# Low-rank decay columns appended to the first head's value weights, with another order of the first loads and splits

## The chip, the cores and the metric

The kernel runs on one NeuronCore of a Trainium2 chip. The metric is the device time of one execution in microseconds (us). The kernel before was timed three times, and its median counts; one further execution was recorded by the hardware profiler, and all views of the trace come from that one. Engines are named as the profile names them: PE (TensorE, with PEld for its weight loads), ACT (ScalarE), DVE (VectorE), POOL (GpSimd) and SP (SyncE, which here only issues DMA transfers).

## The reference

One encoder layer in float32 on 1024 tokens of width 1024. Only the beginning matters here: the norm, the combined input projection and the decays that come from its 32 low-rank columns.

```python
h = rmsnorm(x, norm_mix[l])
proj = h @ w_in[l]
q, k, v, r, lr_f, lr_b, u, g_a, g_b = jnp.split(proj, split_points, axis=-1)
log_a_f = log_sigmoid(lr_f @ w_decay_up_fwd[l] + b_decay_fwd[l]) / GATE_NORMALIZER
log_a_b = log_sigmoid(lr_b @ w_decay_up_bwd[l] + b_decay_bwd[l]) / GATE_NORMALIZER
...
o = o_fwd + o_bwd          # gated linear attention, 4 heads, forward and backward
...
x = x + merged @ w_out[l]
h2 = rmsnorm(x, norm_ffn[l])
gate, up = jnp.split(h2 @ w_ffn_in[l], 2, axis=-1)
x = x + (jax.nn.silu(gate) * up) @ w_ffn_out[l]
return rmsnorm(x, norm_final)
```

q and k are 512 wide (4 heads of 128), v is 1024 wide (4 heads of 256), lr_f and lr_b are 16 wide each.

## The kernel before

**Products.** Float32 accuracy comes from three products of numbers in a shorter format (fp32r). Every operand is split into a high part (`hi`, a cast by ACT) and a low part (`lo`, the difference, by DVE or POOL), by `split_to`; `mm3` then issues hi·hi, hi·lo and lo·hi, and calls `pump`, which lets work that was put aside (splits of coming weights, transposes, norms) be issued between matmuls after so much matmul time. There is no scheduler: each engine runs its instructions in the order in which the program issues them.

**The start.** Tokens come in eight tiles of 128. For each tile `norm_x` squares and sums on ACT, adds epsilon on DVE, takes the power −1/2 on POOL (`rms_scale`) and scales the tile on DVE (`xn`). PE transposes `xn` into banks `tr`; `gain_and_split` then takes each pair of feature blocks out with the gain `g_mix`, hi part `hh` by ACT, lo part `hl` by DVE. These are the feature-major activations `hT`, in two halves of 512 tokens. The gains and biases of all vectors come as 40 rows of 128 numbers (`rows`), loaded by six DMAs, and are turned into columns (`cols`) by one PE transpose (`vps`) and one DVE copy.

**Values of the first head.** `values` makes one token tile: 8 blocks of k, three matmuls each, the stationary operand a token tile of `hT`, the moving one 256 columns of weights (`wh`, `wl`). The weights come in four tiles `raw` of two k blocks each; each is split while the first pairs of features are made, ACT's cast of one raw tile standing between two pairs. The low part of the first is DVE's, those of the other three are POOL's. The loop goes over tiles two at a time, with norms and transposes of later tiles between the matmuls.

**Low-rank columns.** After the eight value tiles come 32 matmuls of 512 columns (line 449): the moving operand is `hh` or `hl` of 512 tokens, the stationary one `lw`, in which the 32 low-rank weight columns stand four times, three times as hi and once as lo. That gives `lrT`, feature-major with 128 rows; its third copy is replaced by its own lo part. `up` holds the up-projections in four bands that fit, so that one product `up`·`lrT` has the hi and lo terms (line 640, used by the attention of each head). Between these 32 matmuls the weights of the first head's q are split. Then come q and k of the first head, 512 tokens a time, its attention, and the rest of the layer.

**Buffers and queues.** All loads are issued by SP, in order. A DMA's completion is counted on one of eight semaphores in turn, so a ninth load waits for the first to have landed. The four `raw` buffers are used again by the weights of q and k, once they are split. PSUM has three banks for matmul results and five for transposes, `z` and others.

Of the kernel before, what the change touches and what calls it, by code (L numbers as in the profile page):

```python
# [10 lines left out]
F32 = mybir.dt.float32  # L11
# [6 lines left out]
P = 128  # L18
# [8 lines left out]
RANK = 16  # L27
CH = 128
# [23 lines left out]
def kernel(  # L52
# [38 lines left out]
    def name(s):  # L91
        count[0] += 1
        return f"{s}_{count[0]}"
# [140 lines left out]

    order = []
# [108 lines left out]
    vec_rows = [(norm_mix, 8), (norm_ffn, 8), (gla_norm, 8), (pool_scale, 8), (b_decay_fwd, 4), (b_decay_bwd, 4)]  # L344
    n_rows = sum(n for _, n in vec_rows)
    rows = tmp.tile([n_rows, P], F32, tag="t2", name="rows")
# [6 lines left out]
    def load_rows(at, v, n):  # L353
        nc.sync.dma_start(rows[at : at + n, :], v[0].rearrange("(j p) -> j p", p=P))
# [6 lines left out]
    load_rows(0, *vec_rows[0])  # L361
    load_x(1)
    for i in range(1, len(vec_rows)):
        load_rows(sum(n for _, n in vec_rows[:i]), *vec_rows[i])
    fetch()
    for t in (2, 3):
        load_x(t)
    nc.sync.dma_start(lraw[:, :, :], w_in[:, LR0:U0].rearrange("(k p) c -> p k c", p=P))
# [20 lines left out]

    lw = [wts.tile([P, 4, 4, 2 * RANK], F32R, tag="wh", name=name("lw")) for _ in range(2)]
    up = slot(F32R, (HEADS, 2, DK), "up")

    def low_rank_weights():
        for i in range(2):
            raw = lraw[:, 4 * i : 4 * i + 4, :]
            nc.scalar.copy(lw[i][:, :, :3, :], raw.unsqueeze(2).broadcast_to([P, 4, 3, 2 * RANK]))
            nc.vector.tensor_tensor(lw[i][:, :, 3, :], raw, as_f32(lw[i][:, :, 0, :]), op=ALU.subtract)  # L400
        nc.scalar.copy(up[:, :, :, :], uraw[:, :, :, :])
        nc.vector.tensor_tensor(up[32:64], uraw[32:64], as_f32(up[32:64]), op=ALU.subtract)
# [8 lines left out]
    nc.tensor.transpose(vps[:, :n_rows], rows[:, :], ident[:n_rows, :n_rows])  # L411
    cols = const.tile([P, n_rows], F32, tag="cols", name="cols")
    nc.vector.tensor_copy(cols[:, :], vps[:, :n_rows])
    g_mix, g_ffn, g_gla, g_pool = (cols[:, 8 * i : 8 * i + 8] for i in range(4))
    b_dec = (cols[:, 32:36], cols[:, 36:40])
# [5 lines left out]
    prepare()  # L421
    for kp, ps in enumerate(trs):
        pending.pop(0)()
        gain_and_split(ps, kp, 0, hT, g_mix)
    w = take(ahead=False)
    norm_x(2)
    norm_x(3)
    for t in range(0, NT, 2):
        if t + 4 < NT:
            begin(norms(t + 4), 1)  # L430
        if t == 2:
            for d, w_up in enumerate((w_decay_up_fwd, w_decay_up_bwd)):
# [6 lines left out]
        values(w, v, t + 1)  # L439
        finish_side()  # L440
        if t == 4:
            low_rank_weights()
    prepare()
    lrT = slot(F32R, (2, HALF), "lrT")
    for half in range(2):
        ps = bank(ps_mm)
        for k in range(KT):
            for i in range(2):
                nc.tensor.matmul(
                    ps[:, :], lw[k // 4][:, k % 4, :, :].rearrange("p a r -> p (a r)"), hT(k, half)[i],  # L450
                    start=k == 0 and i == 0, stop=k == KT - 1 and i == 1,
                )
            pump(2 / 3)
        nc.scalar.copy(lrT[:, half, :], ps[:, :])
        nc.vector.tensor_tensor(lrT[64:96, half, :], ps[64:96, :], as_f32(lrT[64:96, half, :]), op=ALU.subtract)
# [1389 lines left out]
```

## Time and profile before

| | |
|---|---|
| median of three runs | 1403.24 us (1403.14 to 1404.75) |
| the profiled execution's own time | 1401.25 us |
| its span, first to last instruction | 1399.5 us |
| granted TensorE clock, mean | 0.997 |
| DMA traffic | 243.62 MB, mean 174 GB/s |

In the profile a row of a timeline gives start, duration, engine, line, operation, out<-in with the program's names, shape and count; in brackets stands how long the engine had been idle and what ended that. A row of the windows view gives the length of a stretch and the busy time of each engine in it. Line numbers are those of the kernel before.

### The profile page before, as it was taken

To read this page: it belongs to the slowest core of one execution; us is meant where nothing else is said; L and a number is where in the kernel's file an instruction comes from. 1 tells how busy PE (TensorE), PEld (TensorE's weight loads), DVE (VectorE), ACT (ScalarE), POOL (GpSimd) and SP (SyncE) were. 2 spreads that over 40 slices of the span, in tenths; PEclk is the share of its full clock that TensorE was granted. 3 is DMA by queue.
4 is the path that set the end of the run, shared out by engine and by line. 5 is a ranking of instruction groups with operands and counts; after the bars stand their busy time and mean duration, and the time that the engine had idled before them with its cause. 6 is when DMAs were issued, how large, how long until landed. Compare 5 with 4: busy or idle time off the path is not lost.

```text
span 1399.5 us, 18553 instructions
## 1 busy us (share of the span) xinstructions
PE 1369.9 (98%) x6677; PEld 1155.1 (83%) x6677; DVE 843.4 (60%) x1073; ACT 624.1 (45%) x1119; POOL 749.3 (54%) x558
## 2 busy tenths in 40 slices
PE   7999999999999999999999999999999999999997
PEld 6889898988888888788887888888888888888876
DVE  6266757667734885587874865556565556343363
ACT  6364655554333444455346633333333334443253
POOL 3251626142288455568665176666666667454354
PEclk9999999999999999999999999999999999999999
DMA  6212413222377678897424555554444447976461
GB/s 193 76 45 62 136 45 122 91 76 75 122 237 235 208 231 250 317 412 284 157 76 174 172 180 174 173 173 156 144 142 149 140 154 254 387 257 219 165 227 75
DMA packets 167613, 243.62 MB, mean 174 GB/s; under 512 B 10937, under 2 KB 98017, under 8 KB 167521
## 3 DMA queue, kind: packets, MB, share of 16 engines
q1 hardware_dynamic: 155104, 216.23, 46.2%
q10 hardware_dynamic: 12416, 26.22, 5.1%
q8 instruction: 52, 0.85, 0.2%
q14 instruction: 41, 0.33, 0.1%
HBM read 164.55 MB, written 77.86 MB: 173 GB/s over the span
## 4 chain that ended last, share of the span: by engine, by line
PE 69%; DVE 4%; DMA 2%; issue 2%; POOL 2%; ACT 1%; ACTq 0%; SPq 0%; POOLq 0%; DVEq 0%
PE ps L271 67%; DMA u_out<-uph 1%; POOL wl L198 1%; PE tp L959 0%; DMA gor<-g_out 0%; DMA wor<-t_out 0%; DVE upl L585 0%; PE op L800 0%; DMA ph<-p_out 0%; DVE x L1523 0%; PE yb L271 0%; POOL n3rs L1506 0%; POOL mg L1150 0%; POOL gl L1439 0%; ACT wh L197 0%
## 5 line engine op out<-in xcount | busy, mean ns | idle before, releaser
L198 POOL TENSOR_TENSOR wl<-fs,wh 128x512 fp32r<-128x512 f32 x120 | 164.8, 1377 | 165.7 <-ACT wh L197 141.8
L271 PE MATMUL ps<-gl,wh 128*128 128x512 f32 x616 | 239.8, 389 | 0.8 <-DVE gl L1439 0.8
L271 PE MATMUL ps<-gh,wh 128*128 128x512 f32 x616 | 240.3, 390 | 0.0
L271 PE MATMUL ps<-gh,wl 128*128 128x512 f32 x616 | 239.7, 389 | 0.0
L198 POOL TENSOR_TENSOR wl<-fraw,wh 128x512 fp32r<-128x512 f32 x90 | 129.3, 1437 | 65.1 <-ACT wh L197 64.4
L198 POOL TENSOR_TENSOR ol<-gor,oh 128x1024 fp32r<-128x1024 f32 (+1 forms) x42 | 100.2, 2392 | 93.0 <-ACT oh L197 70.3
L271 PE MATMUL ps<-hh,wh 128*128 128x512 f32 x376 | 149.4, 397 | 0.0
L271 PE MATMUL ps<-hh,wl 128*128 128x512 f32 x376 | 146.8, 390 | 0.0
L271 PE MATMUL ps<-hl,wh 128*128 128x512 f32 x376 | 146.5, 390 | 0.0
L198 POOL TENSOR_TENSOR wl<-raw,wh 128x512 fp32r<-128x512 f32 x47 | 64.7, 1391 | 146.4 <-ACT wh L197 135.5
L271 PEld LDWEIGHTS ps<-gl,wh 128*128 128x128 f32 x616 | 115.7, 188 | 24.9 <-DVE gl L1439 1.3
L271 PEld LDWEIGHTS ps<-gh,wl 128*128 128x128 f32 x616 | 115.7, 188 | 24.1
L271 PEld LDWEIGHTS ps<-gh,wh 128*128 128x128 f32 x616 | 115.7, 188 | 23.6
L271 PE MATMUL ps<-oh,oh 128*128 128x512 f32 x308 | 119.9, 389 | 1.1 <-DVE x L1767 1.1
L271 PE MATMUL ps<-ol,oh 128*128 128x512 f32 x308 | 119.9, 389 | 0.2 <-DVE ol L198 0.2
L271 PE MATMUL ps<-oh,ol 128*128 128x512 f32 x308 | 119.8, 389 | 0.0
L198 POOL TENSOR_TENSOR wl<-wraw,wh 128x512 fp32r<-128x512 f32 x56 | 90.2, 1637 | 46.7 <-ACT wh L197 46.6
L198 DVE TENSOR_TENSOR ol<-wor,oh 128x1024 fp32r<-128x1024 f32 (+1 forms) x42 | 61.7, 1489 | 54.0 <-ACT oh L197 45.2
L197 ACT CAST wh<-fs 128x512 fp32r<-128x512 f32 x120 | 73.8, 615 | 31.0 <-DVE fs L869 24.2
L271 PEld LDWEIGHTS ps<-hh,wl 128*128 128x128 f32 x376 | 70.6, 188 | 15.2
L271 PEld LDWEIGHTS ps<-hh,wh 128*128 128x128 f32 x376 | 70.8, 188 | 13.5
L271 PEld LDWEIGHTS ps<-hl,wh 128*128 128x128 f32 x376 | 70.7, 188 | 13.6
(251 smaller groups left out, 3181.1 us busy)
## 6 DMA issues: line engine op xcount, KB each, us to landing
fraw<-in_w_ffn_in_dram SPq DMA_DIRECT2D x44, 512.0 KB, 5.9
gor<-g_out SPq DMA_DIRECT2D x35, 512.0 KB, 6.4
raw<-in_w_in_dram SPq DMA_DIRECT2D x48, 256.0 KB, 3.4
g_out<-s SPq DMA_DIRECT2D x44, 256.0 KB, 2.3
fraw<-in_w_in_dram SPq DMA_DIRECT2D x20, 512.0 KB, 5.4
wor<-t_out SPq DMA_DIRECT2D x20, 512.0 KB
g_out<-g SPq DMA_DIRECT2D x33, 256.0 KB, 2.6
x<-in_x_dram SPq DMA_DIRECT2D x16, 512.0 KB, 5.2
```

The source lines that it names most:

```text
L197: nc.scalar.copy(hi, src)
L198: eng.tensor_tensor(lo, src, as_f32(hi), op=ALU.subtract)
L271: nc.tensor.matmul(ps, a[i], b[j], start=first and n == 0, stop=last and n == 2, skip_group_check=onto)
```

## The change

The 32 low-rank columns are appended to the 256 value columns of the first head. A class `FirstWeights` holds four tile pairs (`fwh`, `fwl`) of two k blocks by 288 columns; `split_values` fills the first 256 columns from `raw`, `split_low` the last 32 from `lraw`, all on POOL. Each value tile is then one product of 288 columns. Its last 32 are copied by ACT, four times side by side, to `low_rows`, token-major. When q has begun, eight transposes (`transpose_low`) bring them into the layout of `lrT`, whose third copy is then treated as before. The 32 matmuls of line 449, `lw` and `low_rank_weights` are gone.

The first weights and the low-rank columns are loaded right after the second x tile, ahead of the third and fourth; the five vectors other than `norm_mix` come after these. `norm_mix` has a transpose of its own (8 columns), the others a second one (32 columns) after the first value tile. All four weight casts stand ahead of the feature scalings on ACT. The low parts of the first two weight tiles are DVE's, those of the other two POOL's. `up` has three bands filled and the fourth left at zero. The first weights of q are fetched in the loop over the tiles and prepared for splitting after tile 5.

```diff
+    class FirstWeights(Weights):
+        def __init__(self, tiles, low):
+            self.per, self.low = 2, low
+            self.todo = tiles
+            self.parts = [tuple(slot(F32R, (2, VL), s) for s in ("fwh", "fwl")) for _ in tiles]
+        def split_values(self, i, eng):
+            split_to(*(t[:, :, :DV] for t in self.parts[i]), self.todo[i][:, :, :], eng)
+        def split_low(self):
+            for i, (hi, _) in enumerate(self.parts):
+                nc.gpsimd.tensor_copy(hi[:, :, DV:], self.low[:, 2 * i : 2 * i + 2, :])
+            for i, (hi, lo) in enumerate(self.parts):
+                nc.gpsimd.tensor_tensor(
+                    lo[:, :, DV:], self.low[:, 2 * i : 2 * i + 2, :], as_f32(hi[:, :, DV:]), op=ALU.subtract
+                )
...
     load_x(0)
-    load_rows(0, *vec_rows[0])
+    load_rows(rows[0], 0, norm_mix, 8)
     load_x(1)
-    for i in range(1, len(vec_rows)):
-        load_rows(sum(n for _, n in vec_rows[:i]), *vec_rows[i])
-    fetch()
+    first_raw = load(*next(order))
+    nc.sync.dma_start(lraw[:, :, :], w_in[:, LR0:U0].rearrange("(k p) c -> p k c", p=P))
     for t in (2, 3):
         load_x(t)
-    nc.sync.dma_start(lraw[:, :, :], w_in[:, LR0:U0].rearrange("(k p) c -> p k c", p=P))
+    for i, (v, n) in enumerate(vec_rows):
+        load_rows(rows[1], sum(n for _, n in vec_rows[:i]), v, n)
...
+    def first_values(w, v, t):
+        ps = bank(ps_mm)
+        for kt in range(KT):
+            mm3(ps[:, :VL], tokens(hT(kt, t // 4), t), w(kt), kt == 0, kt == KT - 1)
+        split_to(*(part[:, t % 4, :] for part in v[t // 4]), ps[:, :DV])
+        nc.scalar.copy(low_rows[:, t, :, :], ps[:, DV:VL].unsqueeze(1).broadcast_to([P, 4, 2 * RANK]))
+    def transpose_low(t):
+        half, i = t // 4, t % 4
+        if i == 0:
+            low_banks[half] = bank(ps_g, "lt")
+        ps = low_banks[half]
+        nc.tensor.transpose(ps[:, i * P : (i + 1) * P], low_rows[:, t, :, :].rearrange("p a r -> p (a r)"), ident[:, :])
+        if i == 3:
+            nc.scalar.copy(lrT[:, half, :], ps[:, :])
+            nc.vector.tensor_tensor(lrT[64:96, half, :], ps[64:96, :], as_f32(lrT[64:96, half, :]), op=ALU.subtract)
...
-    prepare()
+    w = FirstWeights(first_raw, lraw)
+    w.split_low()
+    for i in range(KT // 2):
+        w.split_values(i, nc.vector if i < 2 else nc.gpsimd)
     for kp, ps in enumerate(trs):
-        pending.pop(0)()
         gain_and_split(ps, kp, 0, hT, g_mix)
-    w = take(ahead=False)
...
         if t == 2:
             for d, w_up in enumerate((w_decay_up_fwd, w_decay_up_bwd)):
-                for i in range(4):
+                for i in range(3):
                     load_up(i, d, w_up)
-        values(w, v, t)
+            fetch()
+        first_values(w, v, t)
         finish_side()
+        if t == 0:
+            vectors(1, 8)
...
         if t == 4:
-            low_rank_weights()
-    prepare()
...
-    for half in range(2):
-        ps = bank(ps_mm)
-        for k in range(KT):
-            for i in range(2):
-                nc.tensor.matmul(
-                    ps[:, :], lw[k // 4][:, k % 4, :, :].rearrange("p a r -> p (a r)"), hT(k, half)[i],
-                    start=k == 0 and i == 0, stop=k == KT - 1 and i == 1,
-                )
-            pump(2 / 3)
...
+            up_weights()
+            prepare()
+    soon(1, *(partial(transpose_low, t) for t in range(NT)))
```

SP's queue before, from its fourth load on (`rows` the vectors, `raw` the first weights, `x` token tiles, `lraw` the low-rank columns):

```order
L354 DMA rows<-in_norm_ffn_dram 8x128
L354 DMA rows<-in_gla_norm_dram 8x128
L354 DMA rows<-in_pool_scale_dram 8x128
L354 DMA rows<-in_b_decay_fwd_dram 4x128
L354 DMA rows<-in_b_decay_bwd_dram 4x128
L205 DMA raw_145<-in_w_in_dram 128x2x256
L205 DMA raw_147<-in_w_in_dram 128x2x256
L205 DMA raw_149<-in_w_in_dram 128x2x256
L205 DMA raw_151<-in_w_in_dram 128x2x256
L351 DMA x_128<-in_x_dram 128x1024
L351 DMA x_129<-in_x_dram 128x1024
L368 DMA lraw_136<-in_w_in_dram 128x8x32
```

The same place in the change:

```order
L206 DMA raw_141<-in_w_in_dram 128x2x256
L206 DMA raw_143<-in_w_in_dram 128x2x256
L206 DMA raw_145<-in_w_in_dram 128x2x256
L206 DMA raw_147<-in_w_in_dram 128x2x256
L384 DMA lraw_137<-in_w_in_dram 128x8x32
L371 DMA x_128<-in_x_dram 128x1024
L371 DMA x_129<-in_x_dram 128x1024
L374 DMA rows<-in_norm_ffn_dram 8x128
L374 DMA rows<-in_gla_norm_dram 8x128
L374 DMA rows<-in_pool_scale_dram 8x128
L374 DMA rows<-in_b_decay_fwd_dram 4x128
L374 DMA rows<-in_b_decay_bwd_dram 4x128
```

The weights and `lraw` moved ahead of the x tiles and the vectors; `lraw` is the eighth load and no longer the fifteenth.

POOL before, from the power of the second token tile on (`n1rs` the powers, `wl` low parts of the first weights):

```order
L303 TENSOR_TENSOR n1rs_177<-n1rs_177,half_neg 128x1
L198 TENSOR_TENSOR wl_213<-raw_147,wh_212 128x512
L198 TENSOR_TENSOR wl_223<-raw_149,wh_222 128x512
L198 TENSOR_TENSOR wl_233<-raw_151,wh_232 128x512
L303 TENSOR_TENSOR n1rs_244<-n1rs_244,half_neg 128x1
```

And in the change (`fwh`, `fwl` the widened weights):

```order
L323 TENSOR_TENSOR n1rs_179<-n1rs_179,half_neg 128x1
L249 CAST fwh_204<-lraw_137 128x2x32
L249 CAST fwh_206<-lraw_137 128x2x32
L249 CAST fwh_208<-lraw_137 128x2x32
L249 CAST fwh_210<-lraw_137 128x2x32
L251 TENSOR_TENSOR fwl_205<-lraw_137,fwh_204 128x2x32
L251 TENSOR_TENSOR fwl_207<-lraw_137,fwh_206 128x2x32
L251 TENSOR_TENSOR fwl_209<-lraw_137,fwh_208 128x2x32
L251 TENSOR_TENSOR fwl_211<-lraw_137,fwh_210 128x2x32
L199 TENSOR_TENSOR fwl_209<-raw_145,fwh_208 128x2x256
L199 TENSOR_TENSOR fwl_211<-raw_147,fwh_210 128x2x256
L323 TENSOR_TENSOR n1rs_254<-n1rs_254,half_neg 128x1
```

Between the powers of the second and the third token tile stand eight small operations and two splits, where three splits stood.

PE before, from the end of the last value tile on (`ps_599` that tile, `ps_631` the low-rank product, whose rows go on to 32 matmuls):

```order
L271 MATMUL ps_599<-wh_232,hh_465 128x256
L271 MATMUL ps_599<-wl_233,hh_465 128x256
L271 MATMUL ps_599<-wh_232,hl_466 128x256
L449 MATMUL ps_631<-hh_206,lw_157 128x512
L449 MATMUL ps_631<-hl_207,lw_157 128x512
```

And in the change (`ps_620` the last value tile, `ps_683` the first half of q, `lt` the transposes of the low rows `lr`):

```order
L291 MATMUL ps_620<-fwh_210,hh_482 128x288
L291 MATMUL ps_620<-fwl_211,hh_482 128x288
L291 MATMUL ps_620<-fwh_210,hl_483 128x288
L291 MATMUL ps_683<-hh_228,wh_613 128x512
L291 MATMUL ps_683<-hl_229,wh_613 128x512
L291 MATMUL ps_683<-hh_228,wl_614 128x512
L429 MATMUL lt_687<-ident,lr_158 128x128 x4
L429 MATMUL lt_694<-ident,lr_158 128x128 x4
```

The value matmuls are 288 columns wide, q follows them directly, and the eight transposes stand after q's first three matmuls.

More of the change, by code (lines that the diff above doesn't have):

```diff
@@ L410, with vectors @@
     vps = bank(ps_g, "vps")
[L411 to L415, printed above, removed]
+    cols = [const.tile([P, n], F32, tag=f"cols{n}", name=f"cols{n}") for n in (8, n_rows)]
+    def vectors(i, at):
+        n = cols[i].shape[1]
+        nc.tensor.transpose(vps[:, at : at + n], rows[i][:, :], ident[:n, :n])
+        nc.vector.tensor_copy(cols[i][:, :], vps[:, at : at + n])
+    vectors(0, 0)
+    g_mix = cols[0]
+    g_ffn, g_gla, g_pool = (cols[1][:, 8 * i : 8 * i + 8] for i in range(3))
+    b_dec = (cols[1][:, 24:28], cols[1][:, 28:32])
     norm_x(1)
```

24 lines of the change are left out of this document (10 added, 14 removed).

## The prediction

> **What bounds the kernel now.** I read the page first, for the share of each engine and the chain that ended last.
>
> ```profile
> PE 1369.9 (98%) x6677; PEld 1155.1 (83%) x6677; DVE 843.4 (60%) x1073; ACT 624.1 (45%) x1119; POOL 749.3 (54%) x558
> PE 69%; DVE 4%; DMA 2%; issue 2%; POOL 2%; ACT 1%; ACTq 0%; SPq 0%; POOLq 0%; DVEq 0%
> ```
>
> TensorE (PE) is busy for 98% of the span, so what shortens the time must remove TensorE time or TensorE waiting. The idle rest is 29.6 us (1399.5 less 1369.9). Next the windows view, by stage (values of the first head, the low-rank product, q and k of the first head); after the stretch, a column each for PE, PEld, DVE, ACT and POOL, then clock and DMA.
>
> ```profile
> 10.80:18.70 7.90, 5.70 (x32) 4.61 (x30) 5.28 (x13) 7.87 (x18) 4.89 (x5) 1.00 0.78 235
> 18.70:43.40 24.70, 24.70 (x211) 24.70 (x212) 17.09 (x41) 16.17 (x39) 2.19 (x4) 1.00 0.33 95
> 43.40:50.70 7.30, 7.30 (x34) 6.06 (x33) 1.11 (x2) 2.00 (x4) 2.58 (x2) 1.00 0.14 37
> 50.70:72.90 22.20, 22.20 (x99) 18.40 (x98) 0.69 (x1) 4.66 (x9) 5.08 (x4) 1.00 0.37 107
> ```
>
> From 18.7 to 72.9 us TensorE never idles, with the other engines far below it: each nanosecond taken from its queue there comes off the end. Before 18.7 it waits for others. So the change has two halves: arithmetic on a full engine, and a new order of loads and splits in a stage that others bound.
>
> **The arithmetic.** The low-rank product is 32 matmuls of 512 columns. The timeline gives starts, which I use for pitch, since the busy times of neighbours overlap. These are the first and last of 41 consecutive value matmuls, the first and last of the 32, and what followed.
>
> ```profile
> 38.40 0.28 PE L271 MATMUL ps<-wh,hh 128*128 128x256 f32 x1
> 43.20 0.28 PE L271 MATMUL ps<-wl,hh 128*128 128x256 f32 x1
> 43.44 0.40 PE L449 MATMUL ps<-hh,lw 128*128 128x512 f32 x1
> 50.50 0.39 PE L449 MATMUL ps<-hl,lw 128*128 128x512 f32 x1
> 50.72 0.39 PE L271 MATMUL ps<-hh,wh 128*128 128x512 f32 x1
> ```
>
> Removed: 50.72 − 43.44 = 7.28 us, 0.2275 us each. A 256-column matmul starts every 4.80/40 = 0.120 us.
>
> Added, first term: 8 token tiles x 8 k x 3 products = 192 value matmuls grow from 256 to 288 columns. No row shows 288. The two pitches give a slope of (0.2275 − 0.120)/256 = 0.42 ns a column, so 32 columns cost 13.4 ns and 192 of them 2.58 us. The ends: nothing, if the pitch of 0.120 hides some width, and 192 x (0.2275 − 0.120) = 20.6 us, if 288 cost what 512 do. I take 2.58, since 288 lies close to 256 and a straight line joins the two rows; below nothing is excluded, as a wider matmul streams more columns.
>
> Added, second term: eight 128x128 transposes of the token-major low rows, right after the first three q matmuls. Four such transposes between matmuls look like this:
>
> ```profile
> 33.34 0.29 PE L271 MATMUL ps<-wh,hl 128*128 128x256 f32 x1
> 33.46 0.60 PE L318 MATMUL tr<-ident,xn 128*128 128x128 f32 x4
> 33.81 0.36 PE L271 MATMUL ps<-wh,hh 128*128 128x256 f32 x1
> 34.02 0.28 PE L271 MATMUL ps<-wl,hh 128*128 128x256 f32 x1
> ```
>
> They hold the queue for 0.35 us, and the next matmul takes 0.21 instead of 0.12, so eight in a row cost 2 x 0.35 + 0.09 = 0.79 us. The last one waits for ACT's copy of the last tile's columns, behind that tile's values cast, which before stood here:
>
> ```profile
> 43.64 0.37 ACT L197 CAST vh<-ps 128x256 fp32r<-128x256 f32 x1 [2.51 <-PE ps L271]
> 44.61 1.29 POOL L198 TENSOR_TENSOR wl<-raw,wh 128x512 fp32r<-128x512 f32 x1 [16.94 <-ACT wh L197]
> ```
>
> Cast and copy need about 0.7 us from the last values matmul; three q matmuls (0.68 us) and seven transposes (0.61 us) stand before the transpose that waits, so it is covered.
>
> TensorE's sum: −7.28 + 2.58 + 0.79 = −3.91 us.
>
> The low-rank stage was also cover for splitting q's first weights. The change puts that split into tiles 6 and 7 of the values (24 x 0.133 = 3.2 us each), where POOL is idle (2.19 us busy of 24.70). Its loads go out ahead of tile 2. Cost nothing; without that cover q would wait for one POOL split, 2.5 us by the second row (44.61 + 1.29 − 43.40). The eight ACT copies, the casts of the transposed rows and the split of the up weights lie under 16.17 of 24.70 us of ACT; nothing. SP issues six small uraw loads instead of eight, ahead of weights that nobody awaits; nothing.
>
> **The start.** The next rows are SP's issues, then ACT, DVE, POOL and PE up to where TensorE runs full.
>
> ```profile
> 0.80 0.39 SPq L351 DMA_DIRECT2D x<-in_x_dram  x1
> 2.06 0.34 SPq L354 DMA_DIRECT2D rows<-in_norm_ffn_dram  x1
> 4.51 2.75 SPq L205 DMA_DIRECT2D raw<-in_w_in_dram  x4
> 8.28 0.43 SPq L368 DMA_DIRECT2D lraw<-in_w_in_dram  x1
> 6.38 1.06 ACT L311 ACTIVATE xn<-x 128x1024 f32<-128x1024 f32 x1 [0.72 <-DMA x<-in_x_dram]
> 9.92 0.84 ACT L325 ACTIVATE hh<-tr,cols 128x256 fp32r<-128x256 f32 x2 [0.99 <-PE tr L318]
> 10.64 0.62 ACT L197 CAST wh<-raw 128x512 fp32r<-128x512 f32 x1
> 14.34 1.10 ACT L311 ACTIVATE xn<-x 128x1024 f32<-128x1024 f32 x1
> 15.56 0.15 DVE L302 TENSOR_SCALAR n1rs<-n1ms 128x1 f32<-128x1 f32 x1 [0.16 <-ACT xn L311]
> 11.34 3.79 POOL L198 TENSOR_TENSOR wl<-raw,wh 128x512 fp32r<-128x512 f32 x3 [2.99 <-ACT wh L197]
> 15.80 0.55 POOL L303 TENSOR_TENSOR n1rs<-n1rs,half_neg 128x1 f32<-128x1 f32 x1 [0.67 <-DVE n1rs L302]
> 17.28 0.55 POOL L303 TENSOR_TENSOR n1rs<-n1rs,half_neg 128x1 f32<-128x1 f32 x1 [0.93 <-DVE n1rs L302]
> 18.68 0.44 PE L318 MATMUL tr<-ident,xn 128*128 128x128 f32 x2 [1.04 <-DVE n1rs L302]
> ```
>
> TensorE's full run begins at 18.68 with the transposes of the fourth token tile. Back from there: POOL's power for that tile at 17.28, the power for the third tile at 15.80, DVE's step at 15.56, ACT's square of the third tile at 14.34, which stood behind ACT's interleaved weight casts and feature scalings from 9.92. The two powers and two DVE scalings after 15.80 take 2.88 us and don't change. So **the start moves by as much as POOL's power at 15.80 does**; from the step at 15.56 it could come earlier, but only if POOL is free, and POOL is the point.
>
> ACT first. The four casts now stand before the scalings, in time that ACT spent waiting; without the casts a pair of scalings takes 0.72 us (9.92 to 10.64), so the four pairs end near 9.92 + 2.9 = 12.8, and the step of 15.56 could be at about 14.2. ACT and DVE offer 1.4 us.
>
> POOL now runs eight small operations on the low columns before two splits, and the first of them waits for lraw. When does it land? Bytes moved so far, from windows:
>
> ```profile
> 2.00:4.00 2.00, 0.00 (x0) 0.00 (x0) 2.00 (x4) 0.08 (x1) 1.85 (x28) 1.00 0.84 288
> 4.00:6.00 2.00, 0.00 (x0) 0.00 (x0) 0.86 (x5) 1.15 (x2) 0.00 (x0) 1.00 0.79 249
> 8.00:10.00 2.00, 2.00 (x11) 1.77 (x10) 1.35 (x2) 0.70 (x2) 0.35 (x1) 1.00 1.02 337
> DMA packets 1237, 0.85 MB, mean 341 GB/s; under 512 B 1061, under 2 KB 1061, under 8 KB 1237
> raw<-in_w_in_dram SPq DMA_DIRECT2D x4, 256.0 KB, 3.6
> ```
>
> Ahead of lraw now stand two x tiles and four raw tiles, 2.1 MB; the raw loads go out from 2.06 and not 4.51. With 0.6 MB gone at 4.0 and 337 GB/s after it (the dip to 249 was the late issue), lraw's turn comes near 8.5. The packets row is the stretch 12 to 14.5 of before, in which its 1024 packets of 128 B passed beside other loads: up to 2.2 us. Its bytes alone are 0.13 MB, 0.4 us at 337 GB/s. The completion follows the last bytes by some 0.4 us: the windows add up to both x tiles near 5.9, and the square of the second began at 6.38. So lraw lands between 8.5 + 0.4 + 0.4 = 9.3 and 8.5 + 2.2 + 0.4 = 11.1; I take 10.5, since packets count here more than bytes. Queued behind it on SP are the third and fourth x tile (wanted from 12.8), the five vectors (wanted after the first values tile, 15.9) and the later x tiles (from 15): at 337 GB/s the two x tiles follow within 3.2 us, so nobody waits. Small POOL operations:
>
> ```profile
> L691 POOL TENSOR_TENSOR fac<-fac x16: 190/204/1141, 87.6 to 296.4; 128x4 f32<-128x4 f32 x16
> L303 POOL TENSOR_TENSOR n1rs<-n1rs,half_neg x8: 548/548/554, 6.0 to 27.1; 128x1 f32<-128x1 f32 x8
> ```
>
> Eight at 0.20 (four elements) to 0.55 us (the power) are 1.6 to 4.4 us; 64 elements of a plain operation lie nearer the first, about 0.25: 2.0 us. Two splits are 3.79 x 2/3 = 2.53. With 0.1 us to start, POOL is free at 10.6 + 2.0 + 2.53 = 15.1, and the power moves from 15.80 to about 15.2: **−0.6 us**. Its ends: ACT's offer, −1.4, and 11.2 + 4.4 + 2.53 = 18.1, +2.3. The first values tile ends at 15.1 + 6 x 0.133 = 15.9, still ahead of the fourth tile's transposes. The other vectors' transpose and their column copy come after it, with rows landed by then, inside the same stall: nothing, or their 0.3 us if the stall is gone.
>
> Sum: −3.91 − 0.6 = **−4.5 us**. Against the profiled execution: span 1399.5 to 1395.0, its run 1401.25 to 1396.75. The median of the runs, 1403.24, lies 2.0 us above that run; I carry the difference over: 1398.7 us.
>
> One rule is weighed against a row. Two neighbouring value matmuls while the array had just begun:
>
> ```profile
> 11.93 0.41 PE L271 MATMUL ps<-wl,hh 128*128 128x256 f32 x1
> 12.14 0.41 PE L271 MATMUL ps<-wh,hl 128*128 128x256 f32 x1
> ```
>
> They start 0.21 us apart, against 0.120 later, though the clock column says 1.00. The change leaves TensorE idle from about 10.2 until the low columns are ready, so the slow pace may last longer. The Trainium skill ("TensorE: Matmul & The Clock Gate", "What's actually happening") says that the array runs at half clock until a window of about 3.4 us was busy. By that rule the slow pace could reach past 16.4 us; the trace agrees as to the halving. It is rival 3.
>
> **The rivals.**
> 1. POOL is free early (lraw at 9.3, operations at 0.20): the start gives all of ACT's offer, −1.4. Sum −5.3, 1397.9 us. Chance 0.17. For it: full DMA from 4 us. Against: 128 B packets passed in 2.2 us.
> 2. The low columns are late or dear: start +2.3, sum −1.6, 1401.6 us. Chance 0.09. Against: only the power costs 0.55 a piece. A first call belongs here: POOL's first of L691 took 1.141 against 0.204, so +0.9 us. The Trainium skill ("GPSIMD Engine Reference", "Instruction dispatch") puts the first call of a freshly loaded kernel at about 6 us; by that, an estimate, the sum would be about +1.5 us, and no row here shows it.
> 3. The array stays slow through the second values tile: 24 matmuls at 0.21 x 288/256 = 0.236 instead of 0.133, +2.5, sum −2.0, 1401.2 us. Chance 0.05. Against: the stall before 18.68 swallows the first tile's share.
> 4. **Slower:** a 288-column matmul costs what 512 columns do. Place: all 192 value matmuls; price 20.6 instead of 2.58 us, sum +13.5, 1416.7 us. It decides from a pitch of 0.120 + (7.28 − 0.79 + 0.6)/192 = 0.157 us. Against: pitch has grown by the column between the two rows. Chance 0.03.
> 5. The change doesn't do what it says: the time freed is waited for later (q's weights, the attention chain of the first head, a load). Say 2.5 us of it, the POOL split: sum −2.0, 1401.2 us. Against: no wait of TensorE up to 72.9. Chance 0.06.
>
> **How the numbers follow.** The forecast keeps 0.60. Its own range is −5.1 to −3.6 us, 1398.1 to 1399.6. The range is from 1396.8 (rival 1 with part of the width free) to 1401.6 (rivals 2, 3 and 5 within); rival 4, the far ends of the others and the unforeseen are left out, under 0.2. A measurement of this kernel can tell about 0.2%, 2.8 us, from no change. Faster by more: forecast and rival 1 with a little of the rest, 0.80. Within: rivals 2, 3 and 5, 0.16. Slower by more: rival 4 and the unforeseen, 0.04.
>
> **What would show it.** In the profile after: value matmuls of 288 columns starting 0.133 us apart; no L449 group of old; eight transposes in some 0.7 us; q's first matmul without a wait; POOL's third power near 15.2 and the fourth tile's transposes near 18.1. A pitch above 0.157, a POOL cast that takes microseconds, or lraw's first reader after 12 us would make the prediction wrong.

## The result, and the profile after

The changed kernel takes 1400.09 us (median of 10 runs, 1398.51 to 1400.50). The kernel before takes 1403.39 us beside it (10 runs, 1401.53 to 1406.36). The ratio is 0.9976, with a 95% interval of 0.9968 to 0.9985: 3.3 us faster. Run again beside three of the experiments, the same two kernels gave 0.9984 (0.9974 to 0.9993), 2.4 us. Two of the 17 executions of one kernel below took 1961 and 1963 us at a granted clock of 0.66, and its ratios leave them out. The profiled execution took 1400.29 us with a span of 1398.6, only 0.9 less than the span of 1399.5 before. That gap between profiles and medians is itself a finding, and the last experiments explain most of it.

I begin with the page of the changed kernel, the busy time of each engine, and the windows view over the stretch in which TensorE had been full before.

```profile
PE 1367.3 (98%) x6654; PEld 1152.5 (82%) x6654; DVE 848.1 (61%) x1073; ACT 624.0 (45%) x1125; POOL 751.1 (54%) x565
```

```profile
18.70:43.40 24.70, 23.96 (x184) 23.26 (x184) 15.43 (x38) 14.61 (x40) 2.10 (x4) 1.00 0.32 91
```

TensorE was busy for all 24.70 us of this stretch before. Now it misses 0.74 us, and its weight loads 1.44 us. Nothing in the forecast had it wait here. The timeline of the changed kernel shows the start (ACT, POOL, PE), a regular run of value matmuls, the first waits, and the hand-over to q.

```profile
7.36 1.06 ACT L331 ACTIVATE xn<-x 128x1024 f32<-128x1024 f32 x1 [1.80 <-DMA x<-in_x_dram]
11.29 0.77 POOL L249 CAST fwh<-lraw 128x64 fp32r<-128x64 f32 x4 [1.96 <-DMA lraw<-in_w_in_dram]
13.13 2.55 POOL L199 TENSOR_TENSOR fwl<-raw,fwh 128x512 fp32r<-128x512 f32 x2
15.63 0.56 POOL L323 TENSOR_TENSOR n1rs<-n1rs,half_neg 128x1 f32<-128x1 f32 x1
18.52 0.44 PE L338 MATMUL tr<-ident,xn 128*128 128x128 f32 x2 [0.87 <-DVE n1rs L322]
...
20.82 0.27 PE L338 MATMUL tr<-ident,xn 128*128 128x128 f32 x1
24.00 0.29 PE L291 MATMUL ps<-fwh,hh 128*128 128x288 f32 x1
26.67 0.29 PE L291 MATMUL ps<-fwh,hl 128*128 128x288 f32 x1
31.87 0.40 PE L291 MATMUL ps<-fwh,hh 128*128 128x288 f32 x1 [0.34 <-ACT hh L345]
32.75 0.40 PE L291 MATMUL ps<-fwh,hl 128*128 128x288 f32 x1 [0.35 <-DVE hl L348]
47.11 0.40 PE L291 MATMUL ps<-hh,wh 128*128 128x512 f32 x1
47.81 1.03 PE L429 MATMUL lt<-ident,lr 128*128 128x128 f32 x8
48.60 0.47 PE L291 MATMUL ps<-hh,wh 128*128 128x512 f32 x1
```

Three things are to be read. The 20 intervals from 24.00 to 26.67 are 0.1335 us each: that is the width of 288, as forecast. The first q matmul starts at 47.11 and not at 50.72, and the eight transposes take 48.60 − 47.81 = 0.79 us. But from the fourth token tile's transposes to q pass 47.11 − 18.52 = 28.59 us, where before 43.44 − 18.68 = 24.76 passed up to the low-rank product. Some 165 of the 192 value matmuls lie in it, and 165 x 13.4 ns explain 2.2 us of the 3.83 more; the marks at 31.87 and 32.75 show that the rest is waiting.

What ACT does at that place is seen in the timeline of ACT and DVE, and in the list of waits of ACT from 18.5 to 47.1 us (total, times, longest).

```profile
21.79 0.27 ACT L421 COPY lr<-ps 128x128 f32<-128x128 f32 x1 [3.30 <-DVE vl L199]
21.95 2.30 ACT L345 ACTIVATE hh<-tr,cols 128x256 fp32r<-128x256 f32 x6
...
21.33 0.42 DVE L199 TENSOR_TENSOR vl<-ps,vh 128x256 fp32r<-128x256 f32 x1
```

The first pair of these scalings in the kernel before:

```profile
19.15 0.84 ACT L325 ACTIVATE hh<-tr,cols 128x256 fp32r<-128x256 f32 x2
```

And the waits:

```profile
ACT lr L421 <- DVE vl L199: 10.3, 7, 3.3
```

ACT's copy of a tile's low columns stands idle until DVE has subtracted the same tile's values, which DVE reaches only after three tiles of normalizing: 3.30 us here, 10.3 us over seven tiles. ACT works its queue in order, so the features' scaling (hh) behind the copy starts at 21.95, where it started at 19.15 before; DVE's hl waits for hh, and TensorE for both. Copy and subtraction read the same PSUM bank, and the built program makes the one wait for the other though the columns differ. The Trainium skill ("PSUM — Partial Sum Buffer", "PSUM bank collisions raise a hardware error") says that the back end's scheduler puts a dependency between any two instructions of different engines on one bank and quadrant, reads among them; the row at 21.79 agrees. It is a rule against this change that the prediction didn't weigh. No run shows which step of the build put this wait in.

### The profile page after: what moved, and what is told of

It is laid out like the page before. It is cut to its first block, busy times and chain, and to the rows that moved or that the text cites. A ratio compares the mean times of both kernels' runs of the same rounds, so it can differ in the third digit from the quotient of the medians.

```text
span 1398.6 us, 18511 instructions
## 1 busy us (share of the span) xinstructions
PE 1367.3 (98%) x6654; PEld 1152.5 (82%) x6654; DVE 848.1 (61%) x1073; ACT 624.0 (45%) x1125; POOL 751.1 (54%) x565
## 5 line engine op out<-in xcount | busy, mean ns | idle before, releaser
L199 POOL TENSOR_TENSOR wl<-raw,wh 128x512 fp32r<-128x512 f32 x44 | 61.4, 1411 | 137.7 <-ACT wh L198 135.2
L291 PEld LDWEIGHTS ps<-hl,wh 128*128 128x128 f32 x376 | 70.7, 188 | 13.4
L291 PEld LDWEIGHTS ps<-hh,wh 128*128 128x128 f32 x376 | 70.7, 188 | 13.4
```

The costliest lines, as they stand in the source:

```text
L199: eng.tensor_tensor(lo, src, as_f32(hi), op=ALU.subtract)
L291: nc.tensor.matmul(ps, a[i], b[j], start=first and n == 0, stop=last and n == 2, skip_group_check=onto)
```

## The experiments

The theory at this point: TensorE's arithmetic came as forecast; the copies behind DVE take back some 1.5 us (theory A of the first experiment); the start, set by POOL, gave less than forecast, since the low columns landed later. The rivals: the stalls have another cause, the start hangs on the x tiles, or the time won in front is waited for later. In all comparisons "the first q matmul" stands at 50.72 us before and 47.11 after.

### The copy ahead of the split

```diff
-        split_to(*(part[:, t % 4, :] for part in v[t // 4]), ps[:, :DV])
         nc.scalar.copy(low_rows[:, t, :, :], ps[:, DV:VL].unsqueeze(1).broadcast_to([P, 4, 2 * RANK]))
+        split_to(*(part[:, t % 4, :] for part in v[t // 4]), ps[:, :DV])
```

> ACT's copy of the low columns is issued ahead of the same tile's split of the values, so that it waits for TensorE alone and not for DVE's subtraction; nothing else changes. Theory A (the eight copies, behind DVE, hold up ACT's feature scalings and cost 1.6 us inside the values stage): from 18.5 us on to the first q matmul 27.0 us instead of 28.6, the first q matmul at 45.5 instead of 47.1 us, no wait of TensorE for the features' hh or hl in the values stage, and a median about 1.5 us below the changed kernel's (ratio to the kernel before near 0.9966). Rival B (the stalls have another cause, such as DVE's own load): the first q matmul stays at 47.1, within 0.3 us, the waits for hl stay, ratio 0.9976. Rival C (the stalls go but the time is waited for later): first q matmul at 45.5, ratio 0.9976.

The ratio is 0.9963 (0.9950 to 0.9977), from four executions. The kernel ran again for a profile that can be compared:

> The copy of the low columns ahead of the split of the values, as in the first experiment, whose profiled execution ran at a lowered clock and can't be read past the first microseconds. Theory A: first q matmul at 45.5 instead of 47.1 us, ACT's copy waits for TensorE alone, no wait of TensorE for hh or hl in the values stage, ratio near 0.9966. Rival B (the stalls have another cause): first q matmul at 47.1 within 0.3 us. Rival C (the time is waited for later): q at 45.5, ratio 0.9976.

The ratio of this second set is 0.9970 (0.9960 to 0.9980), beside 0.9984 for the changed kernel on the same chip. The timeline (ACT, then PE):

```profile
23.02 0.27 ACT L420 COPY lr<-ps 128x128 f32<-128x128 f32 x1
...
20.41 0.27 PE L338 MATMUL tr<-ident,xn 128*128 128x128 f32 x1
45.19 0.40 PE L291 MATMUL ps<-hh,wh 128*128 128x512 f32 x1
```

The waits of ACT from 18.5 to 46 us, all of them:

```profile
ACT lr L420 <- PE ps L291: 5.6, 4, 2.3
ACT hh L345 <- PE tr L338: 4.5, 12, 0.4
```

Nothing on ACT waits for DVE any more, and the list has no wait of TensorE from 18.5 to 46 us. From the same transpose to the first q matmul pass 45.19 − 20.41 = 24.78 us, against 47.11 − 20.82 = 26.29 in the changed kernel: 1.51 us, as theory A said. Rival B falls. Rival C falls as well, if less sharply: the ratio went down by 0.0013 and 0.0014 in the two pairs, some 1.9 us. The intervals of these ratios overlap, but in the second pair the medians of the two kernels, beside each other on one chip, are 1398.7 and 1400.8 us.

### The order of the first loads

The old order, with the vectors ahead of the first weights and the low columns behind two more x tiles:

```diff
+    for i, (v, n) in enumerate(vec_rows):
+        load_rows(rows[1], sum(n for _, n in vec_rows[:i]), v, n)
     first_raw = load(*next(order))
-    nc.sync.dma_start(lraw[:, :, :], w_in[:, LR0:U0].rearrange("(k p) c -> p k c", p=P))
     for t in (2, 3):
         load_x(t)
-    for i, (v, n) in enumerate(vec_rows):
-        load_rows(rows[1], sum(n for _, n in vec_rows[:i]), v, n)
+    nc.sync.dma_start(lraw[:, :, :], w_in[:, LR0:U0].rearrange("(k p) c -> p k c", p=P))
```

> The changed kernel with the old order of loads: vectors ahead of the first weights, the low columns after the third and fourth x tile. Theory A (POOL, which waits for the low columns, sets the start): the low columns land near 12.6 us instead of 11.25, POOL's power of the third x tile comes near 17.0 instead of 15.63, the fourth tile's transposes near 19.8 instead of 18.5, and the run is 1.3 us longer than the changed kernel's (ratio near 0.9985). Rival B (the second x tile, which landed 1 us later in the changed kernel because the weights share the DMA, sets the start through ACT): its square goes back to 6.4 from 7.4 us, and the transposes come 0.5 to 1 us earlier, near 17.8, ratio near 0.997.

```profile
6.33 1.06 ACT L331 ACTIVATE xn<-x 128x1024 f32<-128x1024 f32 x1 [0.65 <-DMA x<-in_x_dram]
14.62 0.77 POOL L249 CAST fwh<-lraw 128x64 fp32r<-128x64 f32 x4 [6.33 <-DMA lraw<-in_w_in_dram]
18.95 0.55 POOL L323 TENSOR_TENSOR n1rs<-n1rs,half_neg 128x1 f32<-128x1 f32 x1
...
14.91 0.61 PE L291 MATMUL ps<-fwh,hh 128*128 128x288 f32 x1 [3.81 <-POOL fwh L249]
16.37 0.44 PE L291 MATMUL ps<-fwh,hh 128*128 128x288 f32 x1
20.93 0.44 PE L291 MATMUL ps<-fwl,hh 128*128 128x288 f32 x1
22.19 0.60 PE L338 MATMUL tr<-ident,xn 128*128 128x128 f32 x4
```

The second x tile is back at 6.33 us, and it helps nothing: rival B falls, POOL sets the start. The size was missed. The low columns land at 14.62 (12.6 expected), the first q matmul moves by 3.3 us, and the ratio is 1.0009 (1.0000 to 1.0018), 4.6 us above the changed kernel where 1.3 were expected. From 16.37 to 20.93 the matmuls stand 4.56/19 = 0.24 us apart, so the first tile's 24 matmuls pass at half pace, 24 x 0.107 = 2.6 us dearer: the mechanism of rival 3 of the prediction. Nearly all of it fell into the stall: 2.89 us lie between the power and the fourth tile's transposes in the changed kernel, so here they could have come at 18.95 + 2.89 = 21.84, and TensorE reached them at 22.19. The 3.3 us of q are the delay of the power, 18.95 − 15.63 = 3.32. The other 1.3 us of the 4.6 aren't shown: the profiled execution, 1402.95 us, was the fastest of the eleven and 2.7 us above the changed kernel's profiled one.

Then the low columns ahead of the weights:

```diff
+    nc.sync.dma_start(lraw[:, :, :], w_in[:, LR0:U0].rearrange("(k p) c -> p k c", p=P))
     first_raw = load(*next(order))
-    nc.sync.dma_start(lraw[:, :, :], w_in[:, LR0:U0].rearrange("(k p) c -> p k c", p=P))
```

> The changed kernel with the load of the low columns ahead of the four loads of the first weights. Theory A (POOL sets the start): the low columns are read from about 8.5 instead of 11.29 us, POOL's eight small operations end before the splits can start, and POOL is free at about 14 instead of 15.65; the third tile's power then follows DVE's step at 15.2 to 15.3 instead of 15.63, and the fourth tile's transposes come near 18.1 instead of 18.5: 0.3 to 0.45 us gained, no more, since ACT and DVE stand next. Rival B (the first weights, now 1 us later, take POOL's place as the last to come): no gain, or up to 0.7 us lost. Both are near the limit of the times; the profile tells them apart.

```profile
8.46 2.21 POOL L249 CAST fwh<-lraw 128x64 fp32r<-128x64 f32 x4
15.00 0.55 POOL L323 TENSOR_TENSOR n1rs<-n1rs,half_neg 128x1 f32<-128x1 f32 x1 [0.70 <-DVE n1rs L322]
```

POOL is now done 0.70 us before DVE's step and waits for it: with the low columns early, ACT and DVE set the start, as theory A said, and the first q matmul comes at 46.48, 0.63 us earlier. The 0.63 us alone would show nothing, since the changed kernel itself has q at 46.19 in another execution (below); POOL's wait does. POOL's four casts took 2.21 us and not 0.77: the last three ran beside DVE's scaling and weight splits and took 0.7 us each, not 0.24. That cost nothing here, since POOL waited afterwards. The ratio of 0.9982 (0.9973 to 0.9991) shows no gain in the time.

### 3.6 us of TensorE put in

```diff
+    idle = bank(ps_mm, "idle")
+    for i in range(16):
+        nc.tensor.matmul(idle[:, :], hT(0, 0)[0][:, :P], hT(1, 0)[0], start=i == 0, stop=i == 15)
```

> The changed kernel with 16 matmuls of 512 columns more ahead of q, whose sums nobody reads: 16 x 0.2275 = 3.64 us more of TensorE at the place where the change removed its 7.28. Theory A (time in front reaches the end one to one): the first q matmul at 50.75 instead of 47.1 us and the run 3.6 us above the changed kernel's (ratio near 1.000). Rival B (a later stage that waits for transfers, at 500 to 600 us, takes up part of it): q moves by 3.6 us as well, but the offset is smaller from 600 us on, and the run is only 1.5 to 2.5 us longer (ratio 0.9987 to 0.9994).

```profile
47.42 3.84 PE L490 MATMUL idle<-hh 128*128 128x512 f32 x16
51.09 0.39 PE L291 MATMUL ps<-hh,wh 128*128 128x512 f32 x1
```

The 16 matmuls take 51.09 − 47.42 = 3.67 us and q moves with them. The ratio is 1.0016 (1.0007 to 1.0025), some 5.6 us above the changed kernel's 0.9976: more than the 3.6 of theory A, and far from rival B's 1.5 to 2.5. So the later stage doesn't swallow what comes late, which speaks against "the gain is hidden later"; where the other 2 us come from, the table below shows for one execution.

### Both edits, and the same kernel twice

> Both: the copy ahead of the split, and the load of the low columns ahead of the first weights. If the two add up, the first q matmul comes at 46.48 - 1.6 = 44.9 us, 5.8 us ahead of the kernel before, and the ratio is 0.9960 or less. Rival: the earlier start is given back in the values stage, since then ACT's and DVE's features are what is waited for: q at 45.5 as with the copy alone, ratio 0.9966.

The ratio is 0.9975 (0.9966 to 0.9985) and the first q matmul stands at 45.95: the two don't add up, and neither expectation came. Here the second x tile came at 7.50 us, so that POOL's power waited for DVE until 16.01. The median is 1399.9 us, where the copy alone has 1398.7 on the same chip: the earlier load is no gain.

> The changed kernel again, unaltered, beside the next three on the same chip. It shows how far one kernel's profiled executions differ from each other. Theory A (the stage at 500 to 590 us, which waits for transfers, differs from one execution to the next): the first q matmul at 47.1 us within 0.5, and the offset against the profiled execution of the kernel before, -2.7 us up to 500 us, comes out of that stage at another value than -1.3, anywhere from -3 to 0; ratio of the times 0.9976 within 0.001. Rival B (the change itself brings the loss there): again -1.3, within 0.3.

```profile
6.34 1.06 ACT L331 ACTIVATE xn<-x 128x1024 f32<-128x1024 f32 x1 [0.65 <-DMA x<-in_x_dram]
10.35 0.77 POOL L249 CAST fwh<-lraw 128x64 fp32r<-128x64 f32 x4 [2.04 <-DMA lraw<-in_w_in_dram]
14.70 0.54 POOL L323 TENSOR_TENSOR n1rs<-n1rs,half_neg 128x1 f32<-128x1 f32 x1
```

The same instructions start 0.9 us earlier, up to the first q matmul at 46.19: the loads landed earlier, and theory A's 47.1 within 0.5 was missed. The power of the third tile follows the landing of the low columns by 4.33 to 4.35 us each time (11.29 to 15.63, 10.35 to 14.70, and 14.62 to 18.95 with the old order). The offset (see the table below) out of the late stage is −1.9 us and not −1.3, so the two executions differ by 0.6 where theory A allowed any value and rival B 0.3; by itself that decides little.

### The new start alone

Loads and splits of the changed kernel, with values of 256 columns and the low-rank product of before; the copies, the transposes and POOL's small operations are left out.

```diff
-            mm3(ps[:, :VL], tokens(hT(kt, t // 4), t), w(kt), kt == 0, kt == KT - 1)
+            mm3(ps[:, :DV], tokens(hT(kt, t // 4), t), tuple(p[:, :DV] for p in w(kt)), kt == 0, kt == KT - 1)
...
-    w.split_low()
...
-    soon(1, *(partial(transpose_low, t) for t in range(NT)))
+    for half in range(2):
+        ps = bank(ps_mm)
...
```

> The new start alone: loads and splits of the changed kernel, but values of 256 columns and the 32 low-rank matmuls kept, with POOL's eight small operations, the eight copies and the eight transposes left out (the weights of that product are made as in the kernel before). POOL is then free well ahead of the third tile's power, which follows DVE's step at about 15.2 us; the fourth tile's transposes come near 18.1 us. Theory A (the stalls in the values stage are due to the eight copies): from there to the first low-rank matmul 24.8 us as in the kernel before, so it comes at 42.9 and the first q matmul at 50.2, 0.5 us ahead of the kernel before; ratio near 0.9996. Rival B (the stalls come with the split of q's weights, which now stands in tiles 6 and 7, or with the later vectors): 26.4 us, the first q matmul at 51.8; ratio 1.0007.

```profile
15.66 0.55 POOL L323 TENSOR_TENSOR n1rs<-n1rs,half_neg 128x1 f32<-128x1 f32 x1 [2.14 <-DVE n1rs L322]
18.54 0.44 PE L338 MATMUL tr<-ident,xn 128*128 128x128 f32 x2 [0.98 <-DVE n1rs L322]
43.27 0.39 PE L496 MATMUL ps<-hh,lw 128*128 128x512 f32 x1
50.52 0.39 PE L291 MATMUL ps<-hh,wh 128*128 128x512 f32 x1
```

From the transposes to the product pass 43.27 − 18.54 = 24.73 us, before's 24.76: the split of q's weights and the later vectors cost nothing there, and rival B falls. The product itself is 50.52 − 43.27 = 7.25 us, the term of 7.28. POOL waited 2.14 us for DVE, and still the power came at 15.66 and not at 15.2: the second x tile had landed late (its square at 7.34), and nothing that POOL does could help. The first q matmul thus came 0.2 us ahead of the kernel before and not 0.5. The ratio is 0.9990 (0.9980 to 1.0001), no difference that is clear of noise.

### The kernel before, again

Two further executions of the unaltered kernel.

> The kernel before, unaltered, profiled again. Theory A (the stage at 500 to 590 us differs from one execution to the next, and the first profiled execution of this kernel was a lucky one): against that execution the start stays within 0.5 us, the offset is near 0 up to 500 us and rises by 0.5 to 3 us at the places at 507, 565 and 579 us, to a run near 1403. Rival B (only the changed kernels lose time there): the offset stays within 0.3 us to the end.

> The kernel before a third time, for the same question: Theory A expects another offset out of the stage at 500 to 590 us than in the two executions before, and a run between 1401.5 and 1406; rival B an offset within 0.3 us of zero.

The first repeat took 1404.13 us, the other 1405.08. The timeline and a window of the first repeat:

```profile
18.66 0.69 PE L318 MATMUL tr<-ident,xn 128*128 128x128 f32 x2 [1.05 <-DVE n1rs L302]
19.57 0.41 PE L271 MATMUL ps<-wh,hl 128*128 128x256 f32 x1
19.79 0.41 PE L271 MATMUL ps<-wh,hh 128*128 128x256 f32 x1
22.22 0.60 PE L318 MATMUL tr<-ident,xn 128*128 128x128 f32 x4
```

```profile
18.70:21.70 3.00, 3.00 (x14) 3.00 (x15) 1.71 (x4) 1.21 (x4) 1.10 (x2) 0.50 0.82 281
```

And the first and the third of these transposes in the execution on which the prediction was built:

```profile
18.68 0.44 PE L318 MATMUL tr<-ident,xn 128*128 128x128 f32 x2 [1.04 <-DVE n1rs L302]
20.82 0.38 PE L318 MATMUL tr<-ident,xn 128*128 128x128 f32 x2
```

Both executions reach 18.7 us together. Then the repeat works at half the granted clock (0.50, the column after the busy times) for 3 us, with 19.79 − 19.57 = 0.22 us between value matmuls and not 0.12, and is 22.22 − 20.82 = 1.40 us behind at the third of these transposes. The third execution falls into it a little later and is 1.27 us behind at q, though its transposes had begun 0.33 us earlier (18.35). So my theory A was wrong about the place: the offset is not near 0 up to 500 us, because the kernel before pays the half pace after its stall at 17.2 to 18.7 us in two of three executions, and the one I worked from was the one that didn't. Rival B falls as well, since the offset also rises later. The Trainium skill ("TensorE: Matmul & The Clock Gate", "What's actually happening") says that the window of activity of about 3.4 us which sets the pace runs freely, so that the same kernel falls differently into it; these three executions agree. TensorE was not idle for such a window: its longest wait there was 1.05 us, and from 15.30 to 18.70 it was busy for 1.55 of 3.40 us.

The table gives, for the profiled executions, the start of TensorE's matmuls less the start of the same ones in the first profiled execution of before (median over 25 us), in us:

| execution | q, 50 us | 475 us | 525 us | 600 us |
|---|---|---|---|---|
| before, again | 1.5 | 1.5 | 1.5 | 2.7 |
| before, third | 1.3 | 2.1 | 2.1 | 3.7 |
| changed | −2.7 | −2.7 | −2.0 | −1.3 |
| changed, again | −3.6 | −3.6 | −2.5 | −1.9 |
| copy ahead of the split | −4.6 | −4.7 | −3.3 | −3.0 |
| low columns first | −3.3 | −2.6 | −1.3 | −0.4 |
| 16 matmuls put in | 1.3 | 2.1 | 2.2 | 5.8 |
| new start alone | −0.2 | −0.2 | −0.2 | −2.6 |

At 230 to 245 us the third execution of before, the run with 16 matmuls more and the one with the low columns first lose some 0.8 us, at half pace: matmuls of 256 columns stand 0.21 us apart there and not 0.12. The times diverge again in a stage at 500 to 590 us. The two places with the largest steps, in the timelines of the changed kernel, of before (first execution), of its repeat, and of the new start alone; the number in brackets is the wait ahead of the row:

```profile
504.87 0.50 PE L291 MATMUL ps<-trh,wh 128*128 128x512 f32 x1 [0.40 <-DVE ga L1270]
577.82 0.79 PE L291 MATMUL ps<-trh,wh 128*128 128x512 f32 x1 [3.77 <-ACT ga L1265]
```

```profile
578.83 0.50 PE L271 MATMUL ps<-trh,wh 128*128 128x512 f32 x1 [3.36 <-ACT ga L1232]
```

```profile
581.50 0.76 PE L271 MATMUL ps<-trh,wh 128*128 128x512 f32 x1 [4.14 <-ACT ga L1232]
```

```profile
577.85 0.50 PE L291 MATMUL ps<-trh,wh 128*128 128x512 f32 x1 [2.63 <-ACT ga L1279]
```

The wait of the matmul at about 578 us is 2.63 to 4.14 us in these rows. After 3.77 and 4.14 us the next ones run 0.43 us apart and not 0.23; after 3.36 us they do so from the fifth on; after 2.63 they run at the full pace. The new start alone is the only one of the 13 comparable profiled executions that escapes the half pace there, and that with the shorter wait is its 2.4 us between 525 and 600. The rows at 578.83 and 581.50 are of one and the same kernel, so this belongs to the execution, with one exception: at 507 us (the row at 504.87) each of the six executions that come 2.5 us or more early waits 0.4 to 1.0 us for DVE's ga, and none of the other seven does. That part of a gain in front is given back.

### The second x tile first, and the array kept busy

Both on top of the copy ahead of the split.

```diff
     load_x(0)
-    load_rows(rows[0], 0, norm_mix, 8)
     load_x(1)
+    load_rows(rows[0], 0, norm_mix, 8)
```

> The kernel with the copy ahead of the split, and the second x tile ahead of the first gain vector on the load queue. Theory A (a second x tile that lands late, 6.3 to 7.5 us over the executions so far, moves the start): its square begins at 6.4 us or before, the third tile's power at 14.7 and the fourth tile's transposes at 17.6 or as TensorE comes to them; 0.3 to 0.5 us gained on the first q matmul at 45.2, and a ratio at or just below that of the copy alone (0.997 and 0.9963). Rival B (POOL, through the low columns at 10.9 to 11.3, sets the start whatever x does): power still at 15.2 to 15.6, no gain. Rival C: the gain vector, now 0.4 us later, holds up the features: 0.3 us lost.

```profile
14.78 0.55 POOL L323 TENSOR_TENSOR n1rs<-n1rs,half_neg 128x1 f32<-128x1 f32 x1
```

The second tile's square begins at 6.09 us and the first q matmul comes at 44.73, the 0.46 us of theory A. But POOL still doesn't wait for DVE here: the low columns came at 10.44 us, and the rows don't say whether x or they brought the gain, which is no larger than the 0.9 us between two executions of the changed kernel. The ratio is 0.9969 (0.9957 to 0.9980), not to be told from the copy alone. The copy alone beat both given kernels beside it; this one ran beside the kernel before only.

```diff
+    idle = bank(ps_mm, "idle")
     for t in range(2):
         for kp, ps in enumerate(trs):
             transpose_tile(ps, xn[t], t, kp)
+        for i in range((24, 16)[t]):
+            nc.tensor.transpose(idle[:, i % 4 * P : (i % 4 + 1) * P], ident[:, :], ident[:, :])
```

> The kernel with the copy ahead of the split, and 40 transposes of the identity more, whose result nobody reads: 24 between the transposes of the first and the second x tile, 16 behind them, where TensorE waits. Theory A (the half pace of the first value matmuls, 0.24 us each up to 14.0 to 16.0 us, comes from TensorE's idling before them): the value matmuls start 0.134 us apart from the first or after a few, TensorE reaches the fourth tile's transposes early and waits there for DVE and POOL, near 17.6 to 18.1; 0 to 0.4 us on the first q matmul against 45.2. Rival B (the pace has nothing to do with what TensorE did before): 0.24 us apart for 10 to 17 matmuls again. Rival C: the added transposes delay the first value matmul by up to 1 us, and that reaches q.

```profile
9.04 4.47 PE L463 MATMUL idle<-ident 128*128 128x128 f32 x24
15.88 0.38 PE L291 MATMUL ps<-fwh,hh 128*128 128x288 f32 x1
16.10 0.30 PE L291 MATMUL ps<-fwl,hh 128*128 128x288 f32 x1
16.77 0.29 PE L291 MATMUL ps<-fwh,hh 128*128 128x288 f32 x1
```

From the second matmul on the pitch is (16.77 − 16.10)/5 = 0.134 us, at a time when the kernel with the old order of loads, idle from 11.1 to 14.9, ran at 0.24. So the pace goes with what TensorE did just before (theory A), not with the time since the start. The changed kernel's second execution agrees: its 16 transposes ran without a break from 7.42 to 10.7 us, and its value matmuls were at full pace from 11.69 on. But the 24 added transposes took from 9.04 to 13.35 us, 0.18 us each, and put the second tile's own off by as much as they overran: rival C decides the time, by more than its 1 us: the first value matmul at 15.88 stood at 11.41 with the copy alone, the first q matmul comes at 48.07, and the ratio is 0.9983 (0.9971 to 0.9994).

## Why the prediction was right and where it failed

- **TensorE's sum, −3.91 us: right.** The product was 7.25 us when put back, the pitch of 288 columns 0.1335 us, the transposes 0.79 us, and the q matmul behind them took 0.31 and not 0.23, another 0.08. With it the sum is −3.83.
- **"The eight ACT copies … lie under 16.17 of 24.70 us of ACT; nothing": wrong, and the largest miss.** It counted ACT's busy time and not what each copy waits for. Each waited for DVE's subtraction on the same bank, ACT's queue stood behind it, and TensorE lost 1.51 us.
- **The start, −0.6 us: the bound was right, the size too large.** POOL's power did set it, POOL's small operations took 1.84 us (2.0 forecast), and rival 2's dear first call didn't show. But the low columns came at 10.35 to 11.56 us in the four comparable executions of this start, not at 10.5. They came late where the second x tile did: 10.35, 10.89, 11.29 and 11.56 us go with squares at 6.34, 6.98, 7.36 and 7.79, where before had 5.59 to 6.38. That the loads ahead share the transfers with this tile is a reading of these rows; no run tests it alone. The power moved from 15.80 to 15.63 in the profiled execution, and to 15.37 in the mean of those four (14.70, 15.22, 15.63, 15.93), from a mean of 15.69 in three executions of before. "ACT and DVE offer 1.4 us" fell with it: the step came at 15.15, not at 14.2.
- **"I carry the difference over": wrong in its reason.** The 2.0 us between the profiled execution and the median were no constant. That execution had escaped the half pace at 18.7 us, 1.4 us, and had lost less at 500 to 590 us than its two repeats.
- **Rival 3 had the right mechanism in the wrong kernel.** With the new start the half pace ends by 14 to 16 us, where a stall covers it, or doesn't come at all (changed, again); it catches the kernel before behind its stall. That part of the gain was in no sum.
- **Rival 5 was there in part:** 0.4 to 1.0 us are waited for at 507 us.

The forecast of −4.5 us and the measured −3.3 and −2.4 thus lie near each other by terms of both signs, which is in part luck: −3.91 arithmetic, about −0.3 start, +1.5 copies, some +0.6 late on the mean (against the first execution the changed kernel loses 1.4 and 1.7 us from 475 to 600 us, before 0, 1.2 and 1.6), and a half pace that the kernel before pays in two of three profiled executions, about −1 on the mean. The sum is about −3.1 us. The copies' loss and this half pace, neither of them in the forecast, nearly cancel. How often before pays it over all its runs isn't shown; three profiles are few. The run with 16 matmuls more lost its 3.6 us between 525 and 600 us in three places of its trace: 1.3 us at 564 us, mostly a wait of 0.70 us for a transfer and slower matmuls around it, 1.1 by the longer wait at 579 us (4.48 us and not 3.36), and 1.1 by more matmuls at half pace behind that. Why the waits were longer in this execution stays open.

## What to carry to other kernels

A small operation added to a half-idle engine is free only if what it waits for is there: look up the other readers of its PSUM bank, and issue it ahead of the engine that is late. Profile the kernel before more than once when the question is one of 0.2%, since a single execution can lack a stall that the median has. A load that is moved forward may take its time from the loads next to it, even those issued ahead: look when they land.

## What the runs showed of the hardware that was not expected

- Two reads of one PSUM bank, by ACT and DVE at different columns, ran one after the other in the built program: ACT waited 3.30 us for DVE.
- After a stall TensorE's matmuls ran at half pace for some 3 us in two of three executions of the same program (granted clock 0.50 from 18.7 to 21.7 us in one of them), although no wait before it was longer than 1.05 us. At about 578 us they did so in 12 of 13 executions, after waits of 2.78 to 4.48 us, at once or a few matmuls later, but not after the one of 2.63 us.
- An x tile issued 0.4 us ahead of 1 MB of weights landed up to 1.4 us later than where they were issued from 4.51 us (square at 7.79 at most, 6.38 before), and in one execution no later (6.34).
- POOL's cast of 128x64 took 0.24 us, but 0.7 us where it ran beside DVE's scaling of a tile or its weight splits (both kernels with the low columns first).
